# Expert marks and index products moved to other places in the first units of an expert-choice layer

## The chip, the cores and the metric

The kernel runs on one core of one Trainium2 chip. The metric is the device time of one execution in microseconds (us). The profile is one execution taken by the hardware profiler; its engines are called PE (TensorE, with PEld for its weight loads), DVE (VectorE), ACT (ScalarE), POOL (GpSimd) and SP (SyncE, which here issues the loads).

## The reference

One encoder layer over 1024 tokens of 1024 channels: a mixing part (Fourier group and windowed attention) and a channel part in which 16 experts each pick their own 128 tokens. Only the second matters here:

```python
def expert_choice_moe(h, w_router, w_gate, w_up, w_down):
    cap = CAPACITY_FACTOR * S // N_EXPERTS                      # 128
    aff = jax.nn.softmax(jnp.einsum('bsd,de->bse', h, w_router), axis=-1)
    g, idx = lax.top_k(aff.transpose(0, 2, 1), cap)
    xin = jax.vmap(lambda hb, ib: hb[ib])(h, idx)
    a = jnp.einsum('becd,edf->becf', xin, w_gate)
    u = jnp.einsum('becd,edf->becf', xin, w_up)
    y = jnp.einsum('becf,efd->becd', jax.nn.silu(a) * u, w_down)
    y = y * g[..., None]
    return jax.vmap(lambda yb, ib: jnp.zeros((S, D), yb.dtype)
                    .at[ib.reshape(-1)].add(yb.reshape(-1, D)))(y, idx)
```

All of it is in 32-bit floats, to which the layer's input is then added.

## The kernel before

**Units.** Each expert has three weight matrices of 4 MB, and each is loaded in four pieces of 1 MB. Such a piece, 256 input channels by 1024 columns, is a *unit*; the units of all experts form one list, numbered from 0 in the order in which TensorE uses them: gate and up of expert 0, then for every further expert its gate, the down matrix of the expert before, and its up matrix. Thirteen buffers (`raw`) hold loaded units, and SyncE issues the load of a unit as soon as the buffer that it takes is free.

**Three products for one.** A 32-bit product is made of three faster ones. `split` (lines 86 and 87) writes a rounded copy of a tile with ScalarE (`wh`, `t0h`) and what is left over with VectorE (`wl`, `t0l`); `mm3` (lines 81 to 83) then multiplies high by high, high by low and low by high. The split of a weight unit is called its *cut*. `product` is the work of one unit: it first lets the selection do some of its steps, then has the cut of a unit up to three further on written (`ahead`), and then writes its own 12 matmuls. Units 0 to 5 are not cut; they multiply the loaded weights directly (line 1292), and use the plain transposed rows `xf`.

**From scores to rows.** For each expert, `pos` holds every token's place among the picked ones. `gather_a` writes the *marks* (`oneh`, line 1306), a matrix of ones and zeros made of eight pieces, by comparing `pos` with 1 to 128; VectorE does it for experts 0 to 3, GpSimd for the others. `gather` multiplies the marks by the token numbers and gates on TensorE (line 1313, the *index product*, eight small matmuls into a tile `pt`), turns them into an index on VectorE (line 1317), and has GpSimd gather the 128 rows from memory into `xe` (line 1319). `flip` (line 1339) transposes rows with TensorE, eight blocks into two `pt` tiles, and splits them into the stationary operand of the products. There are only two `pt` tiles, each a PSUM bank, used in turn by flips, index products and a few others. The rows of a gated expert (`hs`, the *Silu rows*: Silu of gate times up) are flipped in the same way, two units into the next expert's gate.

**The selection.** The picks of experts 0 and 1 are found ahead of the units (`choose`). Expert 0's rows are flipped at line 1377. The rest is the generator `selection`: the gates of expert 0 (line 1384), the split of its rows, marks and index product of expert 1, then `thresholds`, a sort on VectorE that ends in a count on TensorE (line 1176) and in `pos` for experts 1 to 15, and last marks and index product of experts 2 and 3. `product` advances this generator by a fixed number of steps ahead of each unit (line 1286), so these numbers, and the `wait(n)` and `while` lines in the generator, set where in the order each piece stands. From expert 4 on the main loop calls `gather_a` and `gather` itself.

**What sets the order.** `in_order` ties the instructions of PE, DVE, POOL, and ACT in this part to the order in which the code writes them. An engine that waits in front of an instruction holds all that is behind it.

Of the kernel before, what the change touches and what calls it, by code (L numbers as in the profile page):

```python
# [45 lines left out]
def block_kernel(ctx: ExitStack, tc: tile.TileContext, t_in, out):  # L46
# [26 lines left out]
    def pt(name="pt"):  # L73
        return ps.tile([128, 512], F32, name=name, tag="pt", bufs=2)
# [5 lines left out]
    def mm3(o, lh, ll, rh, rl, start, stop):  # L80
        PE.matmul(o, lh, rh, start=start, stop=False)  # L81
        PE.matmul(o, ll, rh, start=False, stop=False)  # L82
        return PE.matmul(o, lh, rl, start=False, stop=stop)  # L83

    def split(hi, lo, src, eng=None):
        ACT.activation(hi, src, AF.Copy)  # L86
        return (eng or DVE).tensor_tensor(lo, src, hi.bitcast(F32), op=OP.subtract)  # L87
# [53 lines left out]
    def drain(g):  # L141
        for _ in g:
            pass
# [950 lines left out]
    def load(m=None):  # L1094
        if m is None:
            m = next((i for i in range(len(units_)) if i not in raws), None)
            if m is None:
                return
        src, u = units_[m]
        rp = raw3 if m % NR in HOME3 else raw2 if m % NR in HOME2 else raw1  # L1100
        r = rp.tile([128, 2, D], F32, name="raw", tag="raw")
        if m == HELD:
            POOL.tensor_copy(r[0:1, 0, 0:1], gs[0][2][0:1, 0:1])
        v = src.rearrange("(k p) c -> p k c", p=128)[:, 2 * u:2 * u + 2, :]
        if m == len(units_) - 1:
            for k in range(2):
                SP.dma_start(r[:, k], v[:, k])
        else:
            SP.dma_start(r, v)
        raws[m] = r  # L1110
# [135 lines left out]
    def wait(n):  # L1246
        for _ in range(n):
            yield


    def thresholds():
        c = yield from sort_tiles(OLD, 2)
        R = yield from halve(c)
        R = yield from top(R[:16], bestT, 16)
        dg = rt.tile([16, 16], F32, name="dg")
        DVE.tensor_scalar(dg, ident[:16, :16], R[:, 127:128], None, op0=OP.mult)
        yield from wait(7)
        p = pt()
        PE.matmul(p[:, :16], ones[:16, :128], dg, start=True, stop=True)
        rest = slice(1, NE)  # L1260
        gq = at_least(p[:, 1:16], NT, rest)
        yield from wait(7)
        c = counted(gq, rest)
        DVE.tensor_tensor(pos[:, :, rest], c[:, :NT], c[:, NT:], op=OP.add)
# [11 lines left out]
    step = [0]  # L1276

    def ahead(la):
        first = place[max(step[0], todo[0])]
        while len(cut) <= first + la and len(cut) < len(todo):  # L1280
            cut_unit(2 if len(cut) == len(todo) - 1 else 1)

    def product(acc, xh, xl, la=3, halves=False):
        n = step[0]
        u = n % 4
        drain(itertools.islice(rest, 5 if n < 9 else 3))
        ahead(min(la, 1 + n // 2))
        step[0] += 1
        if n in PLAIN:
            for k in range(2):  # L1290
                for hf in range(2):
                    PE.matmul(acc[hf], xf[:, 2 * u + k, :], raws[n][:, k, hf * 512:hf * 512 + 512],  # L1292
                              start=(u == 0 and k == 0), stop=(u == 3 and k == 1))
            load()
            return
        wh, wl = cut[n]
        for k, hf in ((0, 0), (1, 0), (0, 1), (1, 1)) if halves else ((0, 0), (0, 1), (1, 0), (1, 1)):
            kc = 2 * u + k
            cs_ = slice(hf * 512, hf * 512 + 512)
            mm3(acc[hf], xh[:, kc, :], xl[:, kc, :], wh[:, k, cs_], wl[:, k, cs_], kc == 0, kc == 7)  # L1300

    def gather_a(e):
        shared = 0 if e < 4 else NT
        oneh = wk.tile([128, NT, 128], BF, name="oneh", bufs=1)
        for t in range(NT):
            (POOL if t < shared else DVE).tensor_scalar(oneh[:, t, :], slots, pos[:, t, e:e + 1], None, op0=OP.is_equal)  # L1306
        return oneh

    def gather(e, oneh):
        n = 6 if e else 2  # L1310
        p = pt()
        for t in range(NT):
            PE.matmul(p[:, :n], oneh[:, t, :], aux[:, t, e, :n], start=(t == 0), stop=(t == NT - 1))  # L1313
            if e == 0 and t < NT - 1:
                busy(1, 128)
        idx = wk.tile([128, 1], I32, name="idx", bufs=4)
        DVE.tensor_scalar(idx, p[:, 0:1], p[:, 1:2], None, op0=OP.add)
        xe = wk.tile([128, D], F32, name="xe", bufs=1)
        POOL.indirect_dma_start(out=xe, out_offset=None, in_=h2d,  # L1319
                                in_offset=bass.IndirectOffsetOnAxis(ap=idx[:, :1], axis=0))  # L1320
        gs[e] = idx, None, xe
        if e:
            gates(e, p[:, 2:6])

    def gates(e, p):
        ax = wk.tile([128, 4], F32, name="ax", bufs=2)
        DVE.tensor_copy(ax, p)
        gt = wk.tile([128, 2], F32, name="gt", bufs=4)
        DVE.tensor_tensor(gt[:, 0:1], ax[:, 1:2], ax[:, 2:3], op=OP.add)  # L1329
        DVE.tensor_tensor(gt[:, 1:2], gt[:, 0:1], ax[:, 0:1], op=OP.add)  # L1330
        gs[e] = gs[e][0], gt[:, 1:2], gs[e][2]
# [39 lines left out]
        cut_unit(2)  # L1371
        cut_unit(2)
    xf = wk.tile([128, D], F32, name="ys", bufs=1).rearrange("p (k c) -> p k c", c=128)
    for k0, n in ((0, 2), (2, 2), (4, 4)):
        p = pt()
        for k in range(n):
            PE.transpose(p[:, k * 128:k * 128 + 128], gs[0][2][:, (k0 + k) * 128:(k0 + k + 1) * 128], ident)
        ACT.activation(xf[:, k0:k0 + n], p[:, :n * 128].rearrange("p (a b) -> p a b", b=128), AF.Copy)
    xh, xl = (wk.tile([128, 8, 128], F32R, name=f"t0{x}", bufs=1) for x in "hl")

    def selection():
        p = pt()
        for t in range(NT):
            PE.matmul(p[:, :4], oneh0[:, t, :], aux[:, t, 0, 2:], start=(t == 0), stop=(t == NT - 1))
        gates(0, p[:, :4])
        yield from wait(4)
        split(xh, xl, xf)
        oneh = gather_a(1)
        yield from wait(3)
        gather(1, oneh)  # L1390
        for _ in thresholds():
            yield
        for e in (2, 3):
            while step[0] < 12 * e - 16:
                yield
            o = gather_a(e)
            yield from wait(7)
            gather(e, o)

    rest = selection()  # L1400
    t2 = traced()
    for e in range(NE):
# [97 lines left out]
```

## Time and profile before

| | |
|---|---|
| median of 3 runs | 981.7 us (980.85 to 984.77) |
| the profiled execution, and its span | 983.92 us, 982.1 us |
| PE, DVE, ACT, POOL busy | 95%, 80%, 64%, 42% of the span |
| moved by DMA | 283.98 MB |
| chain that ended last | PE 82%, DVE 9%, ACT 3%, DMA 2% |

The units run from about 404 us to about 972 us. [...] A timeline row is a group of neighbouring instructions: when it starts, how long it takes as a whole, and in brackets how long its engine idled before it and on whom it waited. The matmuls of one group overlap, so a group is a little longer than the distance to the next one.

### The profile page before, as it was taken

The page shows a single profiled execution, that of the slowest core. Times are in us where ns is not written, and L with a number is a line of the kernel's source. Part 1 is how long each engine was busy: PE and PEld are TensorE (multiplying, and loading weights), DVE is VectorE, ACT ScalarE, POOL GpSimd, SP SyncE. Part 2 cuts the span into 40 slices and gives each one's busy share as a digit, 9 for nine tenths or more (in the row PEclk, how much of TensorE's full clock was granted, in tenths as well). Part 3 has the DMA queues.
Part 4 walks back from the last instruction along what each step waited for, and adds up shares of the span by engine and source line. Part 5 has one row for each costly group of instructions (what it writes and reads, how often), then busy time and mean ns, then how long its engine had stood idle before and what let it go on. Part 6 is the DMA issues. An engine that isn't in the chain of part 4 may idle for free.

```text
span 982.1 us, 13289 instructions
## 1 busy us (share of the span) xinstructions
PE 937.9 (95%) x4788; PEld 736.2 (75%) x4788; DVE 787.6 (80%) x1231; ACT 629.2 (64%) x839; POOL 411.5 (42%) x247
## 2 busy tenths in 40 slices
PE   4999999989999999899899999999999999999996
PEld 2678777657777776468788888888888888888885
DVE  1436787788777968988888988998898898889894
ACT  2464533657566653247578777777777777877771
POOL 1007455100000002203449767876976876792201
PEclk9999999989999999999999999999999999999998
DMA  8977556462222248699999999999999999999912
GB/s 283 345 259 269 183 207 223 135 191 81 80 76 93 76 177 317 255 408 408 357 358 409 383 387 404 393 385 385 411 387 388 408 384 388 389 407 384 386 65 44
DMA packets 91787, 283.98 MB, mean 289 GB/s; under 512 B 8156, under 2 KB 25744, under 8 KB 91592
## 3 DMA queue, kind: packets, MB, share of 16 engines
q1 hardware_dynamic: 86856, 266.32, 70.9%
q0 software_dynamic: 4864, 16.80, 6.7%
q8 instruction: 38, 0.62, 0.3%
q14 instruction: 29, 0.24, 0.1%
HBM read 263.79 MB, written 21.40 MB: 290 GB/s over the span
## 4 chain that ended last, share of the span: by engine, by line
PE 82%; DVE 9%; ACT 3%; DMA 2%; issue 1%; SPq 1%; POOLq 0%; POOL 0%; ACTq 0%; DVEq 0%
PE pa L81 17%; PE pa L83 17%; PE pa L82 17%; PE pu L376 6%; PE pt L1339 3%; PE pj L81 2%; PE yp L728 2%; PE pj L82 2%; PE pj L83 2%; DVE ws L123 2%; PE pt L715 2%; PE pa L1292 2%; PE lg L686 1%; DMA raw<-in_w_ada_dram 1%; PE pv L376 1%
## 5 line engine op out<-in xcount | busy, mean ns | idle before, releaser
L87 DVE TENSOR_TENSOR wl<-raw,wh 128x2048 fp32r<-128x2048 f32 (+1 forms) x189 | 422.6, 2267 | 53.9 <-ACT wh L86 52.9
L86 ACT ACTIVATE wh<-raw 128x2048 fp32r<-128x2048 f32 (+1 forms) x189 | 355.4, 1896 | 79.5 <-PE pa L82 62.6
L1306 POOL TENSOR_SCALAR oneh<-tri_f,pos 128x128 bf16<-128x128 f32 x96 | 212.5, 2228 | 15.1 <-PE pt L1313 14.7
L81 PE MATMUL pa<-wh,t1h 128*128 128x512 f32 x384 | 151.4, 394 | 0.0
L83 PE MATMUL pa<-wl,t1h 128*128 128x512 f32 x384 | 149.6, 390 | 0.0
L82 PE MATMUL pa<-wh,t1l 128*128 128x512 f32 x384 | 149.5, 389 | 0.0
L81 PE MATMUL pa<-wh,t0h 128*128 128x512 f32 x360 | 143.2, 398 | 0.0
L82 PE MATMUL pa<-wh,t0l 128*128 128x512 f32 x360 | 140.9, 391 | 0.0
L83 PE MATMUL pa<-wl,t0h 128*128 128x512 f32 x360 | 140.9, 391 | 0.0
L83 PEld LDWEIGHTS pa<-wl,t1h 128*128 128x128 f32 x384 | 72.1, 188 | 15.1
L82 PEld LDWEIGHTS pa<-wh,t1l 128*128 128x128 f32 x384 | 72.1, 188 | 14.3
L81 PEld LDWEIGHTS pa<-wh,t1h 128*128 128x128 f32 x384 | 72.1, 188 | 14.3
L83 PEld LDWEIGHTS pa<-wl,t0h 128*128 128x128 f32 x360 | 68.0, 189 | 14.3
L82 PEld LDWEIGHTS pa<-wh,t0l 128*128 128x128 f32 x360 | 68.0, 189 | 13.7 <-issue 0.2
L81 PEld LDWEIGHTS pa<-wh,t0h 128*128 128x128 f32 x360 | 68.0, 189 | 13.7 <-issue 0.2
L1319 POOL DMA_INDIRECT xe<-h2d,idx x16 | 18.4, 1147 | 136.4 <-DVE gt L1329 122.6
L809 POOL TENSOR_TENSOR rs<-ss,mhalf 128x1 f32<-128x1 f32 x7 | 3.9, 558 | 170.8 <-DVE ss L807 146.8
L1357 POOL DMA_INDIRECT out_dram<-ys,idx x15 | 49.3, 3287 | 45.9 <-DVE ys L1356 41.8
L1354 POOL TENSOR_TENSOR ys<-ys,g_r 128x512 f32<-128x512 f32 x28 | 50.0, 1804 | 43.1 <-ACT ys L1353 43.1
L278 ACT ACTIVATE hf<-pt,sh1c,G1c 128x128 f32<-128x128 f32 (+1 forms) x56 | 22.6, 482 | 35.6 <-PE pt L271 35.6
L376 PE MATMUL pu<-wh,hh 128*128 128x512 f32 x128 | 42.6, 417 | 1.0 <-ACT hh L86 0.9
L689 DVE CUSTOM_DVE_ANT_0 sb<-lg,bias,sink 128x384 f32<-128x384 f32 (+1 forms) x64 | 35.2, 579 | 9.9 <-PE lg L687 4.9
(344 smaller groups left out, 1644.2 us busy)
## 6 DMA issues: line engine op xcount, KB each, us to landing
raw<-in_w_gate_dram SPq DMA_DIRECT2D x64, 1024.0 KB, 9.1
raw<-in_w_up_dram SPq DMA_DIRECT2D x64, 1024.0 KB, 8.9
raw<-in_w_down_dram SPq DMA_DIRECT2D x63, 1024.0 KB, 8.8
raw<-in_w_ada_dram SPq DMA_DIRECT2D x16, 1024.0 KB, 7.6
raw<-in_w_ada_dram SPq DMA_DIRECT2D x16, 512.0 KB, 9.6
xt<-in_x_dram SPq DMA_DIRECT2D x8, 512.0 KB
raw<-in_w_out_dram SPq DMA_DIRECT2D x4, 1024.0 KB, 4.9
raw<-in_x_dram SPq DMA_DIRECT2D x8, 512.0 KB
```

The costliest lines, as they stand in the source:

```text
L81: PE.matmul(o, lh, rh, start=start, stop=False)
L82: PE.matmul(o, ll, rh, start=False, stop=False)
L83: return PE.matmul(o, lh, rl, start=False, stop=stop)
L86: ACT.activation(hi, src, AF.Copy)
L87: return (eng or DVE).tensor_tensor(lo, src, hi.bitcast(F32), op=OP.subtract)
L278: ACT.activation(hf[:, a * w:a * w + w], tp[:, a * w:a * w + w], AF.Identity, scale=G1c[:, kc:kc + 1], bias=sh1c[:, kc:kc + 1])
L376: PE.matmul(acc[:, :c1 - c0], lhs, r[kc][:, c0:c1], start=first, stop=(kc == 7 and r is w_l), skip_group_check=c0 == 1024)
L689: DVE.tensor_tensor_reduce(sb[:, :wid], lg[:, :wid], bias[:, kv * 4 + i, j0:j0 + wid], 1.0, sk[:, i:i + 1], op0=OP.add, op1=OP.max, accum_ ...
L1306: (POOL if t < shared else DVE).tensor_scalar(oneh[:, t, :], slots, pos[:, t, e:e + 1], None, op0=OP.is_equal)
L1339: PE.transpose(p[:, k * 128:k * 128 + 128], src[:, (4 * b + k) * 128:(4 * b + k + 1) * 128], ident)
L1354: POOL.tensor_tensor(ys[:, cs_], ys[:, cs_], g2_r[:, cs_], op=OP.mult)
L1357: POOL.indirect_dma_start(out=out2, out_offset=bass.IndirectOffsetOnAxis(ap=idx[:, :1], axis=0), in_=ys, in_offset=None, compute_op=OP.add)
```

## The change

Four things are written in another order; no operation is added or taken out.

- Ahead of unit 0 stand only the first four flips of expert 0's rows. The other four, the gates of expert 0, the split of its rows and the marks of expert 1 come between units 0 and 1 (`xf_flip(4, 4)` is called in `selection`, and the steps are 0 ahead of unit 0 and 1 ahead of unit 1).
- The index product of expert 1 comes behind unit 1, not behind unit 0, and the sort behind it is spread otherwise among the cuts.
- Marks of expert 2 are written ahead of unit 11, not 10, and its index product stands between units 11 and 12, not between 12 and 13.
- Marks of expert 3 are written ahead of unit 15, not 20, and its index product between units 15 and 16, not between 21 and 22.

```diff
@@ product
-        drain(itertools.islice(rest, 5 if n < 9 else 3))
+        drain(itertools.islice(rest, 0 if n == 0 else 1 if n == 1 else 5 if n < 10 else 3))
@@ ahead of the units
-    for k0, n in ((0, 2), (2, 2), (4, 4)):
+
+    def xf_flip(k0, n):
         p = pt()
         for k in range(n):
             PE.transpose(p[:, k * 128:k * 128 + 128], gs[0][2][:, (k0 + k) * 128:(k0 + k + 1) * 128], ident)
         ACT.activation(xf[:, k0:k0 + n], p[:, :n * 128].rearrange("p (a b) -> p a b", b=128), AF.Copy)
+
+    xf_flip(0, 2)
+    xf_flip(2, 2)
     xh, xl = (wk.tile([128, 8, 128], F32R, name=f"t0{x}", bufs=1) for x in "hl")
     def selection():
+        xf_flip(4, 4)
         p = pt()
...
         gates(0, p[:, :4])
-        yield from wait(4)
         split(xh, xl, xf)
         oneh = gather_a(1)
-        yield from wait(3)
+        yield
         gather(1, oneh)
...
         for e in (2, 3):
-            while step[0] < 12 * e - 16:
+            while step[0] < 7 * e - 6:
                 yield
             o = gather_a(e)
-            yield from wait(7)
+            yield from wait(9 - 2 * e)
             gather(e, o)
```

What this makes of TensorE's order at the start of the units, before (flips at L1377, gates at L1384, units 0 to 5 at L1292, index product of expert 1 at L1313):

```order
L1377 MATMUL pt<-ident,xe 128x128 x8
L1384 LDWEIGHTS oneh
L1384 MATMUL pt<-aux,oneh 128x4
...
L1292 MATMUL pa<-raw,ys 128x512 x4
L1313 LDWEIGHTS oneh
L1313 MATMUL pt<-aux,oneh 128x6
...
L937 MATMUL pt<-ident,aff 32x128
L1292 MATMUL pa<-raw,ys 128x512 x20
```

And in the change (flips at L1378, gates at L1390):

```order
L1378 MATMUL pt<-ident,xe 128x128 x4
L1292 MATMUL pa<-raw,ys 128x512 x4
L1378 MATMUL pt<-ident,xe 128x128 x4
L1390 LDWEIGHTS oneh
L1390 MATMUL pt<-aux,oneh 128x4
...
L1292 MATMUL pa<-raw,ys 128x512 x4
L1313 LDWEIGHTS oneh
L1313 MATMUL pt<-aux,oneh 128x6
...
L937 MATMUL pt<-ident,aff 32x128
L1292 MATMUL pa<-raw,ys 128x512 x16
```

Unit 0 (four matmuls) stands between the two halves of the flips, and the index product of expert 1 has unit 1 in front of it as well.

VectorE's order from the end of the sort (`dg`) to the marks of experts 2 and 3, before (`wl` is a cut, `cn` and `pos` end the count, `t0l` and `t1l` are row splits):

```order
L1256 TENSOR_SCALAR dg<-ident,R 16x16
L87 TENSOR_TENSOR wl<-raw,wh 128x2048
L1424 TENSOR_TENSOR hs<-hs,pa 128x512 x2
...
L87 TENSOR_TENSOR wl<-raw,wh 128x2048 x2
L87 TENSOR_TENSOR t0l<-pt,t0h 128x512 x2
L1179 SCALAR_TENSOR_TENSOR cn_4660<-pa,gq_4588 128x240
L1264 TENSOR_TENSOR pos<-cn_4660 128x8x15
L1306 TENSOR_SCALAR oneh<-tri_f,pos 128x128 x8
L87 TENSOR_TENSOR wl<-raw,wh 128x2048 x3
L1317 TENSOR_SCALAR idx<-pt 128x1
```

And in the change:

```order
L87 TENSOR_TENSOR t0l<-pt,t0h 128x512 x2
L87 TENSOR_TENSOR wl<-raw,wh 128x2048
L1179 SCALAR_TENSOR_TENSOR cn_4678<-pa,gq_4606 128x240
L1264 TENSOR_TENSOR pos<-cn_4678 128x8x15
L1306 TENSOR_SCALAR oneh<-tri_f,pos 128x128 x8
L87 TENSOR_TENSOR wl<-raw,wh 128x2048
L1317 TENSOR_SCALAR idx<-pt 128x1
...
L87 TENSOR_TENSOR wl<-raw,wh 128x2048 x3
L1306 TENSOR_SCALAR oneh<-tri_f,pos 128x128 x8
L87 TENSOR_TENSOR wl<-raw,wh 128x2048
```

Between `dg` and the count there is one cut more than before (three and one, where there were three), and the second group of marks, those of expert 3, follows four cuts later; before, it stood behind the product `hs` of expert 1 (L1424).

TensorE's order at the index product of expert 3 (L1313) and the flips of the Silu rows of expert 1 (L1339, `hs`), before:

```order
L83 MATMUL pa<-wl,t0h 128x512
L1339 MATMUL pt<-ident,hs 128x128 x8
L1313 LDWEIGHTS oneh
L1313 MATMUL pt<-aux,oneh 128x6
...
L81 MATMUL pa<-wh,t0h 128x512
```

And in the change, with the flips of expert 2's rows (`xe`) between the two:

```order
L83 MATMUL pa<-wl,t0h 128x512
L1313 LDWEIGHTS oneh
L1313 MATMUL pt<-aux,oneh 128x6
...
L1339 MATMUL pt<-ident,xe 128x128 x8
...
L1339 MATMUL pt<-ident,hs 128x128 x8
L81 MATMUL pa<-wh,t0h 128x512
```

The index product no longer follows the flips of the Silu rows. On GpSimd, the gather of expert 3's rows (L1319) now stands ahead of the marks of expert 4 (L1306); before, it stood behind them. ScalarE's and SyncE's orders are as before.

## Rows read from the trace of the kernel before

**Rows 1.** The page: its first line.

```profile
span 982.1 us, 13289 instructions
```

**Rows 2.** Stretch: length, busy us of PE, PEld, DVE, ACT, POOL, clock, DMA share, GB/s.

```profile
484.00:960.00 476.00, 476.00 (x2289) 394.50 (x2288) 425.00 (x294) 369.57 (x273) 314.41 (x146) 1.00 0.97 371
```

**Rows 3.** Waits of TensorE from 400 us on: us in total, times, longest.

```profile
PE pt L1313 <- DVE t1l L87: 3.6, 1, 3.6
```

**Rows 4.** Timeline of TensorE, start of the experts: start, us, what [idle before].

```profile
403.32 0.66 PE L1377 MATMUL pt<-ident,xe 128*128 128x128 f32 x4 [0.26 <-ACT ys L1378]
...
404.01 3.68 PE L1292 MATMUL pa<-raw,ys 128*128 128x512 f32 x8
408.67 1.55 PE L1313 MATMUL pt<-aux,oneh 128*128 128x6 bf16 x8 [0.98 <-DVE oneh L1306]
...
410.19 17.33 PE L1292 MATMUL pa<-raw,ys 128*128 128x512 f32 x40
```

**Rows 5.** Timeline of ScalarE, then of VectorE, same place.

```profile
404.64 1.06 ACT L86 ACTIVATE t0h<-ys 128x1024 fp32r<-128x1024 f32 x1
411.21 1.91 ACT L86 ACTIVATE wh<-raw 128x2048 fp32r<-128x2048 f32 x1 [5.52 <-DMA raw<-in_w_gate_dram]
...
407.19 1.22 DVE L87 TENSOR_TENSOR t0l<-ys,t0h 128x1024 fp32r<-128x1024 f32 x1
408.33 1.65 DVE L1306 TENSOR_SCALAR oneh<-tri_f,pos 128x128 bf16<-128x128 f32 x8
```

**Rows 6.** Timeline of VectorE from the sort to the marks, then of TensorE.

```profile
423.12 2.29 DVE L87 TENSOR_TENSOR wl<-raw,wh 128x2048 fp32r<-128x2048 f32 x1 [0.72 <-ACT wh L86]
...
431.37 1.29 DVE L87 TENSOR_TENSOR t1l<-pt,t1h 128x512 fp32r<-128x512 f32 x2 [1.87 <-ACT t1h L86]
...
433.66 2.29 DVE L87 TENSOR_TENSOR wl<-raw,wh 128x2048 fp32r<-128x2048 f32 x1 [0.49 <-ACT wh L86]
...
437.45 4.49 DVE L87 TENSOR_TENSOR wl<-raw,wh 128x2048 fp32r<-128x2048 f32 x2
...
443.80 1.66 DVE L1306 TENSOR_SCALAR oneh<-tri_f,pos 128x128 bf16<-128x128 f32 x8
...
447.16 0.39 PE L81 MATMUL pa<-wh,t0h 128*128 128x512 f32 x1
...
449.88 0.35 PE L1313 MATMUL pt<-aux,oneh 128*128 128x6 bf16 x8
450.09 0.47 PE L81 MATMUL pa<-wh,t0h 128*128 128x512 f32 x1
```

**Rows 7.** Timeline of TensorE, then of VectorE, at expert 3's product.

```profile
475.58 1.04 PE L1339 MATMUL pt<-ident,hs 128*128 128x128 f32 x8
480.19 0.34 PE L1313 MATMUL pt<-aux,oneh 128*128 128x6 bf16 x8 [3.57 <-DVE t1l L87]
...
479.45 1.29 DVE L87 TENSOR_TENSOR t1l<-pt,t1h 128x512 fp32r<-128x512 f32 x2
```

**Rows 8.** Stretches, columns as in rows 2.

```profile
407.70:410.20 2.50, 1.41 (x10) 0.83 (x11) 2.29 (x9) 0.00 (x0) 0.00 (x0) 1.00 1.03 424
...
480.00:482.00 2.00, 1.81 (x12) 1.52 (x12) 1.93 (x7) 0.00 (x0) 1.36 (x2) 0.64 1.01 406
482.00:484.00 2.00, 2.00 (x6) 1.51 (x6) 1.58 (x1) 0.00 (x0) 2.00 (x2) 0.51 1.04 414
```

**Rows 9.** Timeline of GpSimd's marks, and of VectorE beside the second row.

```profile
480.64 8.84 POOL L1306 TENSOR_SCALAR oneh<-tri_f,pos 128x128 bf16<-128x128 f32 x8 [14.72 <-PE pt L1313]
...
513.87 18.51 POOL L1306 TENSOR_SCALAR oneh<-tri_f,pos 128x128 bf16<-128x128 f32 x8
...
519.75 6.83 DVE L87 TENSOR_TENSOR wl<-raw,wh 128x2048 fp32r<-128x2048 f32 x3
```

**Rows 10.** The instructions on tile xe: their DMAs.

```profile
DMA to landing us min/median/max: 4.3/7.5/9.9
```

**Rows 11.** Waits of the SP queue, 500 to 900 us.

```profile
SPq L1109 <- DVE wl L87: 302.1, 126, 4.1
```

## The prediction

> **What bounds the kernel now.** I read the page first, then the stretches, then TensorE's waits, then the engines' own order in time around each wait. The span is 982.1 us [rows 1]. From 484 us to 960 us TensorE is busy in all of its 476 us at full clock [rows 2], so nothing done there by another engine can shorten the program; only work taken off TensorE, or idle time before 484 us, can. The list of TensorE's waits from 400 us on is short: 3.6 us for one row split of VectorE [rows 3], 0.98 us for marks [rows 4], and three smaller ones. The change touches just these places. Call the weight pieces units 0, 1, 2 and so on in TensorE's order: 0 to 3 gate and 4 to 7 up of expert 0, 8 to 11 gate of expert 1, 12 to 15 down of expert 0, 16 to 19 up of expert 1, 20 to 23 gate of expert 2.
>
> **Step A: flips and gates of expert 0 behind unit 0.** The second four flips start at 403.32, the eight gate products follow, and unit 0 starts at 404.01 [rows 4]. In the change unit 0 takes the place of those flips, with the same wait for ScalarE's first copy, so it starts 0.69 us earlier, at 403.32. Five units took 17.33 us [rows 4], 3.47 each, so the second flips start at 406.79, unit 1 at 407.48, and TensorE reaches expert 1's index product (now behind unit 1) at 410.95. That product needs expert 1's marks, which need VectorE to be through with the split of expert 0's rows, which needs the second flips. From the flips' start at 403.32 to the end of ScalarE's half of the split at 404.64 + 1.06 = 405.70 were 2.38 us [rows 4, 5]; so now 406.79 + 2.38 = 409.17. VectorE's half takes 1.14 (407.19 to 408.33) and the marks 1.65 [rows 5]: marks done at 411.96, against 408.33 + 1.65 = 409.98. The next unit started 0.21 us after the last mark (410.19) [rows 4], so unit 2 starts at 412.17. Before, it started at 410.19 + 3.47 = 413.66. **TensorE is 1.49 us ahead, VectorE 1.98 us behind.** ScalarE's next piece, the cut of unit 8, began at 411.21 behind its load [rows 5] and is not touched. Expert 1's gather is issued 2 us later; its rows land within 9.9 us [rows 10], by about 424 us, and are flipped behind unit 6, near 428.6. That hides it.
>
> **Step B: the product of expert 2 stands before unit 12, not behind it.** VectorE carries the lag through the sort. It idled 0.72, 1.87 and 0.49 us there [rows 6], 3.08 in all, waiting for ScalarE, which follows TensorE and so comes up to 1.49 us earlier. Late by 1.98 and released 1.49 earlier are 3.47, more than all this idle, so nearly none of it is left; I keep 0.26 us, an estimate, between none and the 0.49 of the last wait. The cut that began at 433.66 then begins at 433.66 + 1.98 - 3.08 + 0.26 = 432.82. From it to the last mark of expert 2 were 443.80 + 1.66 - 433.66 = 11.80 us [rows 6]; one more cut now stands in front of the count, 4.49/2 = 2.2 us [rows 6]. Marks done at 446.82. TensorE would come to the product at 447.16 - 1.49 = 445.67 [rows 6], waits, and starts unit 12 at 446.82 + 0.21 = 447.03. **The lead of step A is nearly all given back, as a new wait of some 1.2 us.** In the trace the product cost 0.21 us behind unit 12 (449.88 to 450.09), and a unit takes 2.72 us (447.16 to 449.88) [rows 6]; unit 13 starts at 449.75, 0.34 ahead.
>
> **Step C: marks and product of expert 3 between units 15 and 16.** VectorE follows with four cuts (8.8 us), the index group (0.6, an estimate for four instructions on a few columns), a wait for ScalarE and the marks (1.65). The wait: the last of these cuts takes the buffers of unit 13, free at 449.75 + 2.72 = 452.47, and ScalarE needs 1.91 [rows 5], so until 454.38, while VectorE is there at 446.82 + 6.6 + 0.6 = 454.02: 0.36. Marks done at 446.82 + 11.41 = 458.23. TensorE arrives at 449.75 + 3 x 2.72 = 457.91 and goes on at 458.23 + 0.21 = 458.44. In the trace unit 16 began at 450.09 + 3 x 2.72 + 0.1 of refilling = 458.35. So TensorE is now 0.1 us behind where it was, with the third product already paid.
>
> **Step D: the wait that goes.** In the trace the product of expert 3 comes right behind the eight flips of the Silu rows of expert 1 (475.58). Those fill both PSUM tiles of the pt kind; the product needs one back, and VectorE empties them only at 479.45, with marks and two cuts in front. TensorE idles 3.57 us [rows 7]. In the change nothing that needs a pt tile follows these flips until those of expert 3's rows, nine units later, so the wait has no successor, and the next cuts are needed no earlier than 2.72 us apart. The product's own 0.20 us has been paid in step C. [...]
>
> **Sum:** +0.1 - 3.57 - 0.20 - 1.70 = -5.4 us. The profiled execution took 983.92 us, so 978.5 in its terms. It lies 2.2 us over the median of the runs shown, 981.7; none of the four terms depends on that, so the forecast is 981.7 - 5.4 = **976.3 us**.
>
> **What the terms hang on.** Step A's lead is worth at most 1.49 and at least nothing, since step B eats it: if VectorE is quicker than I reckon, the new waits shrink and up to 1.4 us come back. The new waits are not in the trace; the nearest row is the stretch 407.70 to 410.20, where TensorE stood or crawled through the same eight products for 2.5 us and the granted clock stayed at 1.00 [rows 8]. The wait of 3.57 us is the bound on the other side: there it fell. 1.2 us is nearer to the first, so I charge no clock for it; the other end is one fall, 1.7 us, and is kept for the range. Expert 3's gather now stands on GpSimd's queue ahead of expert 4's marks and must wait for the flips of expert 2's rows behind unit 18, at 458.44 + 3 x 2.72 + 1.04 [rows 7] = 467.6; it lands by about 479 [rows 10], some 20 us before its flips behind unit 30.
>
> **Rivals.**
> *No new waits.* VectorE has the marks of experts 2 and 3 ready in time. For it: 1.2 and 0.4 us are small against a path of 45 us. Against it: one whole cut is put in front. Then 1.49 + 3.57 + 1.70 = 6.8 us are gained: 974.9 us.
> *The clock falls at a new wait.* Against it stands the stretch at full clock [rows 8]. Price 1.7: 978.0 us.
> *VectorE is later still*, by one more cut (2.2 us) at the marks of expert 2, with the clock falling once: 5.4 - 2.2 - 1.7 = 1.5 us gained, 980.2 us. For it: its queue has no idle left from the sort to the marks, so any delay arrives in full.
> *The weights set the pace*, and the gain comes back as waits for loads: 981.7 us. For it: the DMA share of 0.97 over the long stretch [rows 2]. Against it: the loads themselves wait for VectorE to free a buffer, 302.1 us of the 400 from 500 us on [rows 11]; they are paced by consumption and run ahead of it.
> *GpSimd blocks VectorE: slower.* Expert 4's marks move on GpSimd from 480.64 [rows 9] to about 469, into a stretch in which VectorE cuts units 22 to 25 without a gap. Were VectorE held for their 8.84 us, the cut of unit 25, ready by my count 3.6 us before TensorE wants it, would be 5.2 us late, and the clock would fall: 5.4 - 5.2 - 1.7 = -1.5, so 983.2 us. It decides from a hold of 7.3 us (3.6 + 5.4 - 1.7) on. Against it: beside 18.51 us of the same marks three cuts took 6.83 us, 2.28 each, as long as one with GpSimd idle (2.29) [rows 6, 9]; it is the marks that stretched, from 8.84 to 18.51 us. [...]
>
> **How the numbers follow.** Forecast (4.6 to 6.2 us gained) 0.57; no new waits 0.12; a clock fall 0.12; VectorE later still 0.08; weights pace it, or nothing happens, 0.05; GpSimd blocks, or another mishap on that side, 0.06. Half a per cent, 4.9 us, is about what a measurement of this kernel can tell from no change, so the border is 976.8 us and lies inside the forecast: two thirds of it and all of the second case are faster by more, 0.38 + 0.12 = 0.50. Slower by more than that takes a hold of well over 10 us: 0.04. The rest, 0.46, is within. The range takes the first four cases, 0.89, with half a microsecond below the best for the spread of runs: 974.4 to 980.4.
>
> **What would show it.** TensorE's wait for the split of the Silu rows near 476 must be gone and the granted clock 1.00 from 476 to 484; unit 0 starts near 403.3 and unit 2 near 412.2; a wait for marks of about 1.2 us stands near 446 and one of a few tenths near 458. Should the wait near 446 be over 3 us, or the clock fall there, step B is wrong; if TensorE waits for cuts between 477 and 490, step D is.

## The result, and the profile after

| | before | changed |
|---|---|---|
| median | 982.47 us, 8 runs (980.85 to 984.77) | 977.56 us, 8 runs (976.06 to 980.19) |
| ratio, 95% interval | | 0.9948 (0.9936 to 0.9960) |
| the profiled execution, and its span | 983.92 us, 982.1 us | 976.06 us, 974.2 us |

The change takes 4.9 us off, where 5.4 were forecast. The ratio times the 981.7 us of the first three runs is 976.6 us, where 976.3 were forecast. The gain is 0.52%, with an interval from 0.40 to 0.64%.

The two spans differ by 7.9 us, more than the medians do. Part of it lies ahead of the change: the first flips of expert 0 start at 400.12 us, where before they started at 402.43. That part is not the change's doing: in a second profiled execution of the changed kernel (the last run below) they start at 402.30. So from here on places are compared after adding 2.31 us (402.43 - 400.12) to the times of the changed kernel; in the text such a sum is called *shifted*. From the first flips on, the two profiled executions differ by about 5.5 us.

First the page, and TensorE's waits from 400 us on (us in total, times, longest), to hold against [rows 1, 3]:

```profile
span 974.2 us, 13290 instructions
```

```profile
PE pt L1378 <- DMA xe<-h2d,idx: 0.9, 1, 0.9
PE pa L1292 <- ACT ys L1379: 0.3, 1, 0.3
```

The 3.6 us for the split `t1l` are gone, and the view names no new wait. That is not the whole truth: a product whose marks arrive one by one shows no idle time, it only gets longer. So I looked at how long those groups take. TensorE's timeline at the start of the units (start, us, what [idle before]), to hold against [rows 4]:

```profile
400.12 0.63 PE L1378 MATMUL pt<-ident,xe 128*128 128x128 f32 x4 [0.94 <-DMA xe<-h2d,idx]
401.00 3.70 PE L1292 MATMUL pa<-raw,ys 128*128 128x512 f32 x8 [0.26 <-ACT ys L1379]
404.54 0.60 PE L1378 MATMUL pt<-ident,xe 128*128 128x128 f32 x4
...
408.69 1.23 PE L1313 MATMUL pt<-aux,oneh 128*128 128x6 bf16 x8
...
409.89 13.90 PE L1292 MATMUL pa<-raw,ys 128*128 128x512 f32 x32
```

And further on, at the products of experts 2 and 3 (line 1313) and the two flips of Silu rows (line 1339, `hs`), to hold against the TensorE rows of [rows 6, 7]:

```profile
436.02 1.34 PE L1339 MATMUL pt<-ident,hs 128*128 128x128 f32 x8
...
443.79 0.96 PE L1313 MATMUL pt<-aux,oneh 128*128 128x6 bf16 x8
444.61 0.47 PE L81 MATMUL pa<-wh,t0h 128*128 128x512 f32 x1
...
455.61 0.58 PE L1313 MATMUL pt<-aux,oneh 128*128 128x6 bf16 x8
456.05 0.47 PE L81 MATMUL pa<-wh,t1h 128*128 128x512 f32 x1
...
473.39 1.03 PE L1339 MATMUL pt<-ident,hs 128*128 128x128 f32 x8
474.19 0.48 PE L81 MATMUL pa<-wh,t0h 128*128 128x512 f32 x1
```

An index product without a wait takes 0.35 us [rows 6]. The three here take 1.23, 0.96 and 0.58, so they stand about 0.9, 0.6 and 0.2 us. Unit 22 follows the flips of the Silu rows at once, at 474.19, shifted 476.50; before it started at 480.39 us, behind a product that itself started at 480.19 [rows 7]. VectorE, which sets those three products (marks at line 1306, split at line 87):

```profile
408.03 1.65 DVE L1306 TENSOR_SCALAR oneh<-tri_f,pos 128x128 bf16<-128x128 f32 x8
...
427.66 1.29 DVE L87 TENSOR_TENSOR t1l<-pt,t1h 128x512 fp32r<-128x512 f32 x2 [0.51 <-ACT t1h L86]
...
442.86 1.66 DVE L1306 TENSOR_SCALAR oneh<-tri_f,pos 128x128 bf16<-128x128 f32 x8
...
452.09 2.29 DVE L87 TENSOR_TENSOR wl<-raw,wh 128x2048 fp32r<-128x2048 f32 x1 [0.37 <-ACT wh L86]
454.30 1.65 DVE L1306 TENSOR_SCALAR oneh<-tri_f,pos 128x128 bf16<-128x128 f32 x8
```

And stretches (length, busy us of PE, PEld, DVE, ACT, POOL, TensorE's granted clock as a share of its full one, DMA share, GB/s): at the product of expert 2, behind the flips of the Silu rows, and the long rest, to hold against [rows 2, 8]:

```profile
443.00:447.00 4.00, 3.95 (x24) 2.91 (x23) 3.96 (x12) 1.92 (x1) 0.00 (x0) 1.00 1.02 409
476.00:478.00 2.00, 2.00 (x11) 1.65 (x10) 2.00 (x4) 1.94 (x2) 2.00 (x4) 1.00 1.02 416
481.70:957.70 476.00, 476.00 (x2290) 394.48 (x2289) 428.52 (x298) 368.79 (x273) 307.04 (x141) 1.00 0.97 370
```

The granted clock stays at 1.00 in all three; before it was 0.64 and 0.51 behind the wait [rows 8]. The long rest is as full of TensorE work as it was.

### The profile page after: what moved, and what is told of

Its sections match the earlier page's. It is cut to its first block, busy times and chain, and to the rows that moved or that the text cites. A ratio compares the mean times of both kernels' runs of the same rounds, so it can differ in the third digit from the quotient of the medians.

```text
span 974.2 us, 13290 instructions
## 1 busy us (share of the span) xinstructions
PE 934.3 (96%) x4786; PEld 733.1 (75%) x4788; DVE 789.2 (81%) x1231; ACT 629.3 (65%) x839; POOL 417.4 (43%) x247
## 4 chain that ended last, share of the span: by engine, by line
PE 79%; DVE 8%; DMA 5%; ACT 4%; issue 2%; SPq 1%; POOL 0%; POOLq 0%; ACTq 0%; DVEq 0%
PE pa L81 17%; PE pa L83 17%; PE pa L82 17%; PE pu L376 4%; PE pt L1339 3%; DVE ws L123 2%; PE pj L82 2%; PE pa L1292 2%; PE pj L81 2%; PE pj L83 2%; PE yp L728 2%; PE pt L715 2%; DMA raw<-in_w_ada_dram 1%; PE lg L686 1%; DMA ws<-in_w_in_dram 1%
## 5 line engine op out<-in xcount | busy, mean ns | idle before, releaser
L1306 POOL TENSOR_SCALAR oneh<-tri_f,pos 128x128 bf16<-128x128 f32 x96 | 217.9, 2284 | 0.5
L1319 POOL DMA_INDIRECT xe<-h2d,idx x16 | 17.8, 1111 | 135.0 <-DVE gt L1329 117.6
```

## The experiments

The question left by a right forecast is whether it was right for its reasons: does the gain come from expert 3's move alone, what exactly in that move makes it, and where does the lead of the new start go? Times are told as the difference that the ratio makes of 982 us; for the change itself that is 5.1 us. The runs were made in groups on several chips, each beside the kernel before, and the changed kernel was run again only beside the last one. In the traces I measure two places from the start of the first flips of expert 0: the start of unit 22, and that of the index product of expert 4 (line 1313, between units 31 and 32), by when the clock is back at 1.00 (in the kernel before from 484 us on).

| | to unit 22 | to expert 4's product |
|---|---|---|
| before | 77.96 us (402.43 to 480.39) | 107.78 us (to 510.21) |
| changed | 74.07 us (400.12 to 474.19) | 102.27 us (to 502.39) |

So the changed kernel is 3.89 us ahead at unit 22 and 5.51 us ahead at expert 4's product; the 1.62 us between the two are the clock.

### Only the move of expert 3

The kernel before, with this in `selection`:

```diff
-        for e in (2, 3):
-            while step[0] < 12 * e - 16:
+        for e, s, w in ((2, 8, 7), (3, 15, 3)):
+            while step[0] < s:
                 yield
             o = gather_a(e)
-            yield from wait(7)
+            yield from wait(w)
```

> The kernel before, with one part of the change: marks of expert 3 ahead of unit 15 and its index product between units 15 and 16; the start of the units and expert 2 stay as before. Theory (step D carries the gain): the wait of 3.57 us, the 1.70 us of lower clock and the product's own 0.20 us behind the Silu rows' flips go, and the product is paid again between units 15 and 16, with a wait for the marks. By the trace of before VectorE reaches these marks behind five cuts from 445.46 us on, the last of them released by unit 13 at about 457, so the marks end near 458.7 and unit 16 starts near 459.0 instead of 458.35: 0.5 to 1.1 us lost there. Sum -4.4 to -5.0 us against before, clock 1.00 from 476 to 484. Rival (the start order carries the gain): within 1 us of before.

Measured: 978.5 us, ratio 0.9950 (0.9934 to 0.9966), 4.9 us gained, as much as the whole change. The marks came a little late, as expected, and nothing was left to wait for behind the Silu flips:

```profile
458.09 0.58 PE L1313 MATMUL pt<-aux,oneh 128*128 128x6 bf16 x8
...
475.87 1.03 PE L1339 MATMUL pt<-ident,hs 128*128 128x128 f32 x8
476.66 0.48 PE L81 MATMUL pa<-wh,t0h 128*128 128x512 f32 x1
```

Unit 16 started at 458.53, 56.29 us from the first flips (402.24); by the prediction's count it was 55.92 before (458.35 - 402.43), so 0.37 us were lost there, a little less than the 0.5 to 1.1 expected. Unit 22 is at 74.42, expert 4's product (504.87) at 102.63: 5.15 us ahead. The theory holds: step D carries the gain.

### Only the new start

The changed kernel with expert 3 put back. With these numbers the index product of expert 2 stands between units 12 and 13 again, too, so that it has no wait here:

```diff
-        for e in (2, 3):
-            while step[0] < 7 * e - 6:
+        for e, s, w in ((2, 8, 7), (3, 20, 7)):
+            while step[0] < s:
                 yield
             o = gather_a(e)
-            yield from wait(9 - 2 * e)
+            yield from wait(w)
```

> The changed kernel with expert 3 put back: marks ahead of unit 20, index product behind the flips of the Silu rows and unit 21 (and expert 2's product between units 12 and 13 as before). So it is the new start order alone. Theory: TensorE comes up to 1.5 us earlier to the flips of the Silu rows, but the product still waits there for VectorE's row split, and the clock falls as before; the lead shows only as far as VectorE, too, is let go earlier: 0 to -1.5 us against before, with a wait of 3.5 to 5 us at line 1313. Rival (the start order carries the gain): -4 us or more, with no wait there.

Measured: 982.16 us, ratio 0.9991 (0.9979 to 1.0003), 0.9 us gained. The wait is there again, and so is the low clock; first TensorE's wait, then the stretches behind it:

```profile
PE pt L1313 <- DVE t1l L87: 3.6, 1, 3.6
```

```profile
480.00:482.00 2.00, 2.00 (x8) 1.58 (x7) 1.97 (x3) 0.00 (x0) 2.00 (x2) 0.67 1.02 408
482.00:484.00 2.00, 2.00 (x6) 1.51 (x6) 0.49 (x1) 0.81 (x1) 2.00 (x3) 0.50 1.02 410
```

Unit 22 is at 76.86 (402.44 to 479.30), 1.10 us earlier than before. So the lead is not swallowed by this wait, as one could have thought: VectorE and TensorE both come 1.1 us earlier, and the wait keeps its 3.56 us. Alone, the start is worth about a microsecond in the trace; the interval of the times does not exclude nothing. Together with expert 3's move it adds nothing that the times show (4.9 against 5.1 us).

### What in the move matters: marks, product, or gather

The move of expert 3 does three things: the marks leave VectorE's queue in front of the split of the Silu rows; the product no longer needs a `pt` tile behind the flips; and GpSimd gathers the rows ahead of expert 4's marks. The first run below takes the product back and leaves the marks where the change puts them.

```diff
-        for e in (2, 3):
-            while step[0] < 7 * e - 6:
+        for e, s, w in ((2, 8, 5), (3, 15, 21)):
+            while step[0] < s:
                 yield
             o = gather_a(e)
-            yield from wait(9 - 2 * e)
+            yield from wait(w)
```

> The changed kernel with one part put back: the index product of expert 3 stands again behind the flips of the Silu rows and unit 21, while its marks stay ahead of unit 15. Theory (place of the product, by its pt tile, is what counts): the row split that frees the tile comes 0.5 to 2.5 us earlier than before since the marks no longer stand in front of it, so a wait of 2 to 3 us is left, and the clock falls as before or a little less: -0.5 to -2.5 us against before. Rival (the marks in front of the split made the wait): no wait over 1 us, -5 us or more against before.

Measured: 981.36 us, ratio 0.9987 (0.9977 to 0.9996), 1.3 us gained. The wait shrank by 1.0 us and is still the longest; there is a second one, for expert 3's rows:

```profile
PE pt L1313 <- DVE t1l L87: 2.6, 1, 2.6
...
PE pt L1339 <- DMA xe<-h2d,idx: 0.7, 1, 0.7
```

So the marks in front of the split are not what made the wait. The run with the new start alone is the one to compare with. There the marks stood in front, and the split (`t1l`) began 75.93 us behind the first flips (478.37 - 402.44); here it began at 75.91 (478.26 - 402.35), no earlier. The wait is shorter because TensorE came to the flips of the Silu rows later, 73.03 us behind the first flips instead of 72.06, and unit 22 is at 76.83 here, at 76.86 there. One point of the expectation failed: the clock did not fall here (1.00 in every stretch from 476 to 510 us), though TensorE stood 2.56 us.

The next run moves nothing at all. In the kernel before, the product of expert 3 alone goes to one of the six accumulator tiles:

```diff
     def gather(e, oneh):
         n = 6 if e else 2
-        p = pt()
+        p = pa() if e == 3 else pt()
```

> The kernel before with nothing moved; the index product of expert 3 alone is written to one of the six accumulator tiles (pa) instead of one of the two pt tiles. Theory (the wait of 3.57 us is for a pt tile that the Silu rows' flips hold until VectorE's split reads it, and for nothing else): marks were done at 475.1 us, TensorE comes at 476.4, so no wait, clock 1.00 from 476 to 484: -3.57 - 1.70 = -5.3 us against before, as much as the whole change. Rival (the product would have waited for VectorE anyway, or TensorE meets its next cut late instead): a wait of 2 us or more at line 1313 or at lines 81 to 83 before 490 us, and -2 us or less.

Measured: 981.42 us, ratio 0.9985 (0.9974 to 0.9996), 1.5 us gained instead of 5.3. The wait at the product was gone as expected (unit 22 at 74.09, 3.87 us ahead), and the clock was 1.00 from 476 to 484. But 27 us later TensorE stood where it never had. TensorE's wait, GpSimd's timeline, and the stretches behind the wait:

```profile
PE pt L1339 <- DMA xe<-h2d,idx: 2.2, 1, 2.2
```

```profile
475.29 18.96 POOL L1306 TENSOR_SCALAR oneh<-tri_f,pos 128x128 bf16<-128x128 f32 x8 [10.99 <-PE pa L1313]
494.40 1.04 POOL L1319 DMA_INDIRECT xe<-h2d,idx  x1 [0.16 <-issue]
```

```profile
502.00:504.00 2.00, 2.00 (x11) 1.81 (x12) 2.00 (x2) 1.34 (x3) 0.00 (x0) 0.71 0.97 338
504.00:506.00 2.00, 2.00 (x6) 1.51 (x6) 2.00 (x4) 1.56 (x1) 0.00 (x0) 0.50 1.05 281
506.00:508.00 2.00, 2.00 (x16) 1.49 (x15) 2.00 (x2) 0.79 (x1) 0.00 (x0) 0.93 1.05 266
```

GpSimd's marks of expert 4 wait for the product of expert 3. With the product earlier, the marks start while VectorE cuts without a pause, and stretch to 18.96 us; before they had 8.84 us [rows 9], and VectorE stood idle for 3.14 of these, waiting for ScalarE. The gather of expert 3's rows stands behind them, is issued at 494.40, and its rows arrive 2.20 us after TensorE wants to flip them. Then the clock falls: 2 x 0.29 + 2 x 0.50 + 2 x 0.07 = 1.72 us. The sum is 3.57 + 1.70 - 2.20 - 1.72 = 1.35 us gained; measured 1.5. My theory had the wait right and the gain wrong: the rival "TensorE meets something else late" is what happened, though not at a cut.

That makes a prediction: with the gather ahead of those marks the whole gain must appear. The same kernel, with the marks of expert 4 written two units later:

```diff
-        p = pt()
+        p = pa() if e == 3 else pt()
...
-            if u == 0 and 1 < e < NE - 2:
+            if u == (2 if e == 2 else 0) and 1 < e < NE - 2:
                 oneh = gather_a(e + 2)
```

> The kernel before with two edits: expert 3's index product in a pa tile, where it stands, and GpSimd's marks of expert 4 written behind the gather of expert 3's rows (at unit 22 instead of 20). The tile alone had given -1.5 us: the wait at the product was gone, but TensorE then stood 2.2 us at the flips of expert 3's rows, which GpSimd had gathered behind 18.96 us of marks, and the clock fell there. Theory (the change gains by both, the tile and the gather that stands ahead of the marks): no wait at either place, clock 1.00 from 476 to 510, -5.0 to -5.6 us against before. Rival (the later marks of expert 4 make a new wait at its index product behind unit 31, or the weights set the pace): -1 to -3 us, with a wait of 1 us or more at line 1313 near 505 us or for loads.

Measured: 977.82 us, ratio 0.9948 (0.9933 to 0.9962), 5.1 us gained. GpSimd's timeline, and the flips of expert 3's rows on TensorE, now without a wait:

```profile
481.46 0.99 POOL L1319 DMA_INDIRECT xe<-h2d,idx  x1 [15.21 <-DVE gt L1329]
482.49 21.86 POOL L1306 TENSOR_SCALAR oneh<-tri_f,pos 128x128 bf16<-128x128 f32 x8
```

```profile
501.56 1.03 PE L1339 MATMUL pt<-ident,xe 128*128 128x128 f32 x8
```

The clock was 1.00 from 470 to 510 us. (In this one profiled execution it had fallen to 0.50 ahead of unit 0, so I count from the start of unit 1, behind the wait for marks, 410.55 against 410.19 [rows 4]: expert 4's product at 94.64 against 100.02, 5.38 us ahead.) With start, marks and product all where the kernel before has them, a PSUM tile and the order of two GpSimd operations give a gain that the times do not tell from that of the whole change.

### Where the lead of the start goes

Two edits of the changed kernel, each at one of the new waits. The changed kernel itself was not run beside them, and its intervals (0.9936 to 0.9960 at first, 0.9914 to 0.9948 in the last run below) overlap with theirs. So the times of the next three runs settle nothing against it; what is said of where time went rests on one traced execution of each. First, the product of expert 2 one unit later:

```diff
-        for e in (2, 3):
-            while step[0] < 7 * e - 6:
+        for e, s, w in ((2, 8, 8), (3, 15, 3)):
+            while step[0] < s:
                 yield
             o = gather_a(e)
-            yield from wait(9 - 2 * e)
+            yield from wait(w)
```

> The changed kernel with the index product of expert 2 one unit later, between units 12 and 13; its marks stay ahead of unit 11. Theory (the lead of the start is lost at the two new waits, 0.6 us of it here): that product takes 0.34 us instead of 0.96, unit 13 starts 0.6 us earlier, and the wait for the marks of expert 3 grows by 0.2 us, since VectorE had only 0.37 us of idle left: 0.3 to 0.6 us below the changed kernel, about -5.5 us against before. Rival (VectorE's chain alone sets the marks of expert 3, so the time saved comes back at its product): no difference from the changed kernel, -5.1 us against before, and the group at line 1313 near 456 grows by 0.6 us.

Measured: 977.41 us, ratio 0.9938 (0.9923 to 0.9954), 6.1 us gained; not to be told from the changed kernel. In the trace unit 13 came 0.73 us earlier than in the changed kernel (448.87 - 402.28 = 46.59, against 447.44 - 400.12 = 47.32), of which 0.1 is given back behind the product (448.87 to 449.19 from the first matmul to the second, 0.32 us, where the next ones are 0.23 apart); 0.6 were expected. But unit 22 is at 74.72, 0.65 us later than in the changed kernel. The last of the eight small matmuls of expert 3's product stood 1.12 us, for marks that took 2.75 us instead of 1.65, beside a multiply on GpSimd:

```profile
458.82 0.18 PE L1313 MATMUL pt<-aux,oneh 128*128 128x6 bf16 x1 [1.12 <-DVE oneh L1306]
```

```profile
456.01 2.75 DVE L1306 TENSOR_SCALAR oneh<-tri_f,pos 128x128 bf16<-128x128 f32 x8
```

```profile
457.42 4.70 POOL L1354 TENSOR_TENSOR ys<-ys,g_r 128x512 f32<-128x512 f32 x2 [4.99 <-ACT ys L1353]
```

In this trace the rival comes nearer than the theory: what one wait gave back came in at the next. But the traced execution took 978.81 us and was the slowest of the six; whether the marks meet the multiply in the others, no run shows. Second, the marks of expert 1 ahead of the row split on VectorE:

```diff
         gates(0, p[:, :4])
-        split(xh, xl, xf)
         oneh = gather_a(1)
+        split(xh, xl, xf)
         yield
```

> The changed kernel with the marks of expert 1 written ahead of the row split of expert 0 on VectorE, so that they fill its idle of 0.98 us before that split. Theory (step A's wait at the product of expert 1 is VectorE's order): the product takes 0.34 us instead of 1.23, unit 2 starts 0.9 us earlier, VectorE is about 0.95 us earlier too, and both keep it: 0.5 to 0.9 us below the changed kernel, about -5.8 us against before. Rival (VectorE waits for ScalarE or loads further on in the sort, and the new waits at the products of experts 2 and 3 eat it): no difference, -5.1 us, with the groups at line 1313 near 444 and 456 longer by 0.5 us or more.

Measured: 976.76 us, ratio 0.9937 (0.9923 to 0.9951), 6.2 us gained, by the times no more than the run before it. The marks now fill the idle time in which VectorE waited for ScalarE, and the product finds them ready (VectorE, then TensorE):

```profile
406.96 1.65 DVE L1306 TENSOR_SCALAR oneh<-tri_f,pos 128x128 bf16<-128x128 f32 x8
```

```profile
409.84 0.34 PE L1313 MATMUL pt<-aux,oneh 128*128 128x6 bf16 x8
```

Unit 22 is at 73.20 (401.26 to 474.46), 0.87 us ahead of the changed kernel, nearly all of the 0.89 that the product got shorter. Both edits together:

```diff
-        split(xh, xl, xf)
         oneh = gather_a(1)
+        split(xh, xl, xf)
...
+        for e, s, w in ((2, 8, 8), (3, 15, 3)):
```

> The two edits before this one together: marks of expert 1 ahead of the row split, and the index product of expert 2 between units 12 and 13. Theory (the gains add): 0.9 to 1.5 us below the changed kernel, -6 to -6.6 us against before; of the start's lead only the wait at the product of expert 3 is left, 0.3 to 0.8 us. Rival (the wait for the marks of expert 3 takes all of it): -5.1 to -5.5 us, with 1 us or more at line 1313 near 455.

Measured: 976.35 us, ratio 0.9935 (0.9921 to 0.9949), 6.4 us gained. Unit 22 is at 72.73 (402.39 to 475.12), 1.34 us ahead of the changed kernel; of the lead only this is lost:

```profile
456.37 0.73 PE L1313 MATMUL pt<-aux,oneh 128*128 128x6 bf16 x8
```

Here the marks of expert 3 came ahead of GpSimd's multiply and took 1.65 us, so the edit that gave nothing in its own trace gave 0.5 us in this one.

Last, all of it in one kernel (the edits against the changed kernel), and the changed kernel beside it on the same chip:

```diff
-        p = pt()
+        p = pa() if e == 3 else pt()
...
-        split(xh, xl, xf)
         oneh = gather_a(1)
+        split(xh, xl, xf)
...
+        for e, s, w in ((2, 8, 8), (3, 20, 7)):
...
-            if u == 0 and 1 < e < NE - 2:
+            if u == (2 if e == 2 else 0) and 1 < e < NE - 2:
```

> All that the runs so far point to, on the changed kernel: marks of expert 1 ahead of the row split, index product of expert 2 between units 12 and 13, and expert 3 as in the run with tile and gather (marks ahead of unit 20, product behind the Silu flips but in a pa tile, GpSimd's gather ahead of the marks of expert 4). Theory (the lead of the start lives only where no product waits for marks): the 0.4 us that are left of the wait at expert 3's product, between units 15 and 16, go too; unit 22 starts 72.0 to 72.6 us behind the first flips of expert 0 (77.96 before, 74.07 in the changed kernel), -6.5 to -7.5 us against before, 1.5 to 2 us below the changed kernel on the same chip. Rival (the lead meets VectorE's row split of the Silu rows, needed at unit 24, which has the marks of expert 3 in front of it again): a wait of 0.5 us or more at lines 81 to 83 or 1313 between 470 and 490, and no gain over the changed kernel.

> The changed kernel once more, beside the run before it on the same chip, to compare the two directly: -4.9 to -5.4 us against before; unit 22 starts 74.1 us behind the first flips of expert 0. If it comes out within 1 us of the run before it, the lead of the start is worth nothing in time.

Measured: 976.51 us (975.07 to 976.61), ratio 0.9915 (0.9900 to 0.9931); the changed kernel 977.97 us (975.85 to 980.04), ratio 0.9931 (0.9914 to 0.9948), beside 983.99 us for the kernel before. So by the ratio the changed kernel gained 6.8 us here and this one 8.3, both more than expected; for the changed kernel the interval overlaps the first one. Unit 22 is at 72.26 (401.76 to 474.02) against 74.05 (402.30 to 476.35), expert 4's product at 100.46 against 102.26: 1.8 us ahead in the traces, 1.5 us in the medians. The direction is the one expected; the two intervals overlap, so the times alone do not settle it. This kernel is 0.85% (0.69 to 1.00) below the kernel before.

## Why the prediction was right

**What bounds the kernel.** Right: in every run the time gained is idle time of TensorE or lower clock that went, and all of it lies ahead of 510 us: from expert 4's product to the end of the span it is 471.8 to 472.3 us in all twelve traces.

**Step A** was right to a few hundredths. Shifted, unit 0 starts at 403.31 (forecast 403.32), unit 1 at 407.49 (407.48), marks are done at 411.99 (411.96), unit 2 starts at 412.20 (412.17). Each length had been taken from a row of the same instruction, and only the order was new.

**Step B** had the mechanism right and one term missing. VectorE came out as forecast: marks of expert 2 done at 442.86 + 1.66 = 444.52, shifted 446.83 (forecast 446.82). An agreement this close is luck: the idle that it had left at `t1l` was 0.51 us, not 0.26, but from the marks of expert 1 to the cut behind the sort its work without that idle took 20.35 us (430.54 - 409.68 - 0.51) instead of the 20.60 that the prediction took over from before (433.66 - 409.98 - 3.08), and the two errors cancel. The cut on VectorE:

```profile
430.54 2.27 DVE L87 TENSOR_TENSOR wl<-raw,wh 128x2048 fp32r<-128x2048 f32 x1
```

TensorE came later than forecast: its product started at 446.10 instead of 445.67, so it stood 0.6 us, not 1.2. Of the 0.43 us, 0.30 were lost at the flips of the Silu rows of expert 0: 1.34 us instead of the usual 1.04. The eight traces with the new start show 1.31 to 1.34 there, the four with the old one 1.03 or 1.04. By the order of the program the reason is that the second of the two `pt` tiles was held by the result of line 1259, which VectorE reads one cut later than before. The trace fits: VectorE's second read of it (line 1188) ended at 436.58, 0.56 us after the flips had begun; before, it ended at 437.53, 2.2 us ahead of them. But no run took that away, so it is argued. It is the same kind of wait as the one that step D removes, and the prediction did not look for it. It did no harm, since TensorE had to wait for the marks anyway: unit 12 started at 446.92 (forecast 447.03).

**Step C**: marks of expert 3 done at 455.95, shifted 458.26 (forecast 458.23), wait of VectorE for ScalarE 0.37 us (forecast 0.36), unit 16 at 458.36 (forecast 458.44). So at unit 16 nothing of the lead was left, as forecast.

**Step D**: unit 22 came 3.89 us earlier, where 3.67 follow from the forecast's terms (3.57 + 0.20 - 0.10), and the clock stayed at 1.00. The sum's 1.70 us for it are worked out from the 0.64 and 0.51 of [rows 8], 2 x 0.36 + 2 x 0.49; no run shows that figure itself, and between the two places the traces show 1.62. That it is this step which carries the gain is shown by the two runs with the one part and the other: 4.9 us and 0.9 us.

**What the prediction did not see** is why the wait has no successor. It argued with the `pt` tile and the cuts, and mentioned GpSimd's new order only to show that it does no harm. The run with the accumulator tile shows how much hangs on that order: with the marks ahead of the gather, 3.9 of the 5.3 us come back as a wait for expert 3's rows and a fall of the clock. Had the change left GpSimd's order as it was, the same argument could have been wrong by as much; no run tried just that.

**The rivals.** GpSimd's marks of expert 4 did move into VectorE's dense cutting, and it was the marks that stretched, as [rows 9] had suggested; the cuts beside them kept their 2.3 us:

```profile
465.63 2.42 POOL L1319 DMA_INDIRECT xe<-h2d,idx  x1 [1.33 <-PE pt L1339]
468.09 14.31 POOL L1306 TENSOR_SCALAR oneh<-tri_f,pos 128x128 bf16<-128x128 f32 x8
```

```profile
471.74 4.62 DVE L87 TENSOR_TENSOR wl<-raw,wh 128x2048 fp32r<-128x2048 f32 x2
```

The weights did not set the pace: the long rest is 476.00 us of work in 476.00. The clock did not fall at the new waits (1.00 in all stretches from 443 to 482). That was forecast, but the reason given for it, a length nearer to 2.5 us without a fall than to 3.57 with one, does not hold as a rule (below); so this part was in some measure luck. And "no new waits" would have been worth 1.4 us more; the kernel with all edits, 1.8 us ahead in the traces, shows that as much was to be had.

## What to carry to other kernels

A wait is removed only when the next one behind it is known: follow each consumer of the moved result on every queue (here the PSUM tile on TensorE, and the gather on GpSimd) until something has slack, and count the gain from there. Two PSUM tiles shared in turn by flips and small products made an index product wait 3.57 us for a reader that has nothing to do with it; before moving work about, try another tile. And a lead of TensorE lasted here only to its next meeting with an engine that had not gained as well (1.46 us at unit 2, shifted 412.20 against 413.66 by the prediction's count, and none at unit 16), so look for idle time of that engine which the moved work could fill.

## What the hardware showed that I had not expected

**Length alone does not tell whether the clock falls.** TensorE stood 3.57 us and the clock fell to 0.64 and 0.51 in two stretches [rows 7, 8]; it stood 2.56 us (product late, marks early) and the clock stayed at 1.00; it stood 2.20 us (accumulator tile) and the clock fell to 0.71, 0.50 and 0.93 in three stretches, 1.72 us of work. And in the run with tile and gather it fell to 0.50 ahead of the first flips, where no wait of TensorE was longer than 0.41 us (columns as in [rows 2]):

```profile
398.00:400.00 2.00, 1.23 (x8) 0.76 (x8) 1.64 (x8) 0.00 (x0) 1.59 (x3) 0.81 0.00 0
400.00:402.00 2.00, 2.00 (x18) 1.05 (x19) 1.72 (x13) 0.00 (x0) 1.77 (x5) 0.50 0.77 225
```

What decides, no run here shows.

**VectorE, too, took longer beside GpSimd.** In the changed kernel two of VectorE's smallest instructions, 0.16 us each elsewhere, took 0.94 and 1.22 us beside a multiply on GpSimd (timelines of VectorE, then of GpSimd):

```profile
458.39 0.94 DVE L1329 TENSOR_TENSOR gt<-ax 128x1 f32<-128x1 f32 x1
459.36 1.22 DVE L1330 TENSOR_TENSOR gt<-gt,ax 128x1 f32<-128x1 f32 x1
```

```profile
455.89 4.67 POOL L1354 TENSOR_TENSOR ys<-ys,g_r 128x512 f32<-128x512 f32 x2 [7.83 <-ACT ys L1353]
```

That is 1.84 us of VectorE's time, hidden in slack, and the multiply took 4.67 us instead of the 3.56 to 3.61 of the kernel before; in the run with the product of expert 2 moved, the marks took 2.75 us instead of 1.65 beside the same multiply, and TensorE stood 1.12 us for them. Beside GpSimd's marks, on the other hand, the cuts lost next to nothing: no cut in the changed kernel took more than 2.42 us, against 2.29 with GpSimd idle, and in the run with the accumulator tile six of them took 13.66 us. Nor does one order of start fit all that took longer. In the changed kernel a cut that began at 455.87, 0.02 us ahead of the multiply, took its usual 2.28 us, and it was the small instructions, begun while the multiply ran, that took longer. But in the run with the product of expert 2 moved, the last of the eight marks began 0.04 us ahead of the multiply (457.42) and took 1.38 us instead of 0.28; and in the run with the accumulator tile a cut began 0.34 us ahead of two multiplies, while the gather issued at 494.40 still ran, and took 5.04 us instead of some 2.28 (that last mark, then that cut, then the multiplies beside the cut):

```profile
457.38 1.38 DVE L1306 TENSOR_SCALAR oneh<-tri_f,pos 128x128 bf16<-128x128 f32 x1
```

```profile
495.14 5.04 DVE L87 TENSOR_TENSOR wl<-raw,wh 128x2048 fp32r<-128x2048 f32 x1 [1.86 <-ACT wh L86]
495.48 2.54 POOL L1354 TENSOR_TENSOR ys<-ys,g_r 128x512 f32<-128x512 f32 x2
```

What decides there, no run here shows.
